# A decoder layer with hierarchical experts on one core: experts' buffers moved to multiples of 256 bytes, gathers that leave out filling rows, and LayerNorm rows kept on the chip

## The chip, the cores and the metric

The kernel runs on one core of one Trainium2 chip. The metric is the device time of one execution in microseconds (us). The kernel before took 1173.28 us as the median of 3 runs, which lay between 1173.1 and 1176.18 us. The engines are named as in the profile: PE (matrix products; PEld is its weight loading), DVE (vectors), ACT (activations), POOL, and SP, which here mostly starts transfers.

## The reference

One layer of a decoder takes one step for 512 rows of a prompt and for 32 rows of samples (8 sequences of 4): 544 rows of width 1024, all in fp32. Cut to what matters:

```
z = x @ w_in + b_in
A = mLSTM(z)          # 4 heads, chunks of 64 tokens; projection w_a
B = window attention  # 16 query heads, window 128; projection w_b
merge = (sigmoid(g_a) * A + sigmoid(g_b) * B) @ w_out
x = LN1(alpha * x + merge)
x = LN2(alpha * x + MoE(x))
x = LN3(alpha * x + sigmoid(x @ w_pg) * (p @ w_pp))

MoE(x): top-1 of 4 groups, then top-2 of the 8 experts in the group
  y += weight * ((silu(xb @ w_gate[e]) * (xb @ w_up[e])) @ w_down[e])
```

There are 32 experts. Each has a gate matrix and an up matrix of 1024 x 512 and a down matrix of 512 x 1024, 2 MB each, so 6 MB an expert. The 544 rows choose two experts each: 1088 rows pass through experts. `ln_g` and `ln_b` hold the gain and the shift of the three norms, three rows of 1024 (4 KB) each.

## The kernel before

**The stages.** The first 610 us of the span are the dense part: the projections, the two mixers and the merge. Its weights come through a ring of buffers in a pool on the right side of SBUF (`stage`), and each product runs as three products of rounded parts (L612 to L614). A planner orders this part and the tail, from a simulated time line and from hints (`tc.issue_after`). From 610 to 653 us the routing is made: scores, the chosen experts, and for every chosen row a *place*. From 653 to 1081 us the experts run, in `expert_phase`. The rest, to 1173 us, is the tail: the experts' results are gathered back, LN2, the embedding gate and LN3 follow.

**Places and items.** An expert's rows fill items of 32 places, and the last item of an expert is filled up. With these inputs there are 50 items. The routing makes `tok`, an int32 tile of 128 x 20: column g holds the token of each of the 128 places of items 4g to 4g+3. It comes out of matmuls (`At` times `Bf`, the latter holding `tokid`, the token's number), and a place that only fills an item gets the sum zero and so token 0. One gather (`gather_rows`, L228, on POOL) reads the 128 rows of four items from `x1d` in DRAM into `xg`; the first gather, L1968, stands ahead of the stage and reads by column 0 of `tok`.

**The expert stage.** Here the order on every engine is written by hand, with semaphores, in one critical section that the planner doesn't touch. There are four weight slots (`NB = 4`). Slots 0 and 1 are the tiles `w0` and `w1` on the left side of SBUF. Slot 2 is `w2a` on the left with two tiles on the right, slot 3 lies on the right and uses `r_p` for its down matrix. A slot's tile `W0` or `W1` is 12 rows of 1024 floats wide, and after the experts its rows hold other things (`row(W1, i)`).

- SP loads for each expert the gate and up matrices in halves and the down matrix in halves (L127, L133), as the slots come free.
- POOL gathers four items' rows, and stores the results of each item into `ybuf` in DRAM (L234).
- PE transposes the four items' rows (L263) into `psX`; for each item it makes gate and up products (L270), transposes h (L275), and makes the down product (L284).
- ACT applies LN1's gain and shift to the transposed rows (L370, from `gcol`), and Silu (L383). DVE copies the item's columns to `xT` (L413), multiplies h, copies hT (L418) and the result `ysb` (L425).

**Behind the last expert.** SP ends its list with the loads in `late`, one list per slot, each behind the slot's last down product (L202): half of the gate weights `w_pg` into slot 0 (2 MB, semaphore `al`), the rows of `ln_g` and `ln_b` into row 4 of slot 1 (`gb_rows`, six partitions of 4 KB, semaphore `gr`), and the four tiles of the norm's input back into `r_p` (4 x 512 KB, semaphore `rb`). PE then spreads four of these six rows over 128 partitions, each in two halves of 512 columns: a matmul with a column of the identity broadcast over 128 columns as weights (L360). It waits for `gr` first, and from the third half on for ACT's copy out of the bank two halves before (L398). DVE applies gain and shift to the first two tiles of `r_p` (L476), after the `sc` counts of their copies. The stage ends when PE, ACT, DVE and POOL have each counted up `fin`, and the loads of `al` and the stores have landed.

**The tail.** POOL gathers the results of tile 0 and tile 1 (`gather`, L1993), and SP loads the second half of `w_pg` behind the first of these. DVE splits `w_pg` into two parts (`split_from`, L2147). `affine` multiplies a tile by LN1's gain and adds its shift (L2021, L2022); `moe_norm(t)` adds the two experts' results to tile t (`both_rows`, L2026 and L2027) and normalises; `turn(t)` transposes; `embed_norm(t)` makes the gate product and LN3. The spreads of LN3's gain and shift run there too (L2008), from the same six rows.

Of the kernel before, what the change touches and what calls it, by code (L numbers as in the profile page):

```python
# [9 lines left out]
F32 = mybir.dt.float32  # L10
# [3 lines left out]
I32 = mybir.dt.int32  # L14
# [5 lines left out]
P = 128  # L20
# [31 lines left out]
def _layout(parts):  # L52
    off, o = {}, 0
    for name, n in parts:
        off[name] = (o, o + n)
        o += n
    return off, o
# [3 lines left out]
UP32, UP128 = 1.5 * 2.0 ** 28, 1.5 * 2.0 ** 30  # L61


KEEP, KEEP_N = _layout([
    ("ident", 128), ("delta", 32), ("tri", 128), ("iota", 128), ("valid", 5), ("tokid", 5), ("pcol", 1),
    ("turns", 16),
# [17 lines left out]
def _constants():  # L84
    keep = np.zeros((P, KEEP_N), np.float32)
    mix = np.zeros((P, MIX_N), np.float32)
    rel = np.zeros((NB_REL, REL_N), np.float32)

    def put(a, off, name, v):
        lo, hi = off[name]  # L90
        v = np.asarray(v, np.float32)
        a[: v.shape[0], lo:hi] = v

    p, f = np.arange(P)[:, None], np.arange(P)[None, :]
    put(keep, KEEP, "ident", p == f)
    put(keep, KEEP, "delta", (p % NS) == np.arange(NS)[None])
    put(keep, KEEP, "tri", p < f)
    put(keep, KEEP, "iota", np.broadcast_to(f, (P, P)))
    t5 = np.arange(5)[None, :]
    ok = (t5 < 4) | (p < NS)  # L100
    put(keep, KEEP, "valid", ok)
    put(keep, KEEP, "tokid", np.where(ok, t5 * P + p, 0))
    put(keep, KEEP, "pcol", p)
    put(keep, KEEP, "turns", np.broadcast_to(NB * np.arange(16)[None], (P, 16)))
    put(mix, MIX, "cmask", np.where(p <= f, 0.0, BIG))
    s, l = p % NS, np.arange(NS)[None]
    put(mix, MIX, "cmasks", np.where((s // ST == l // ST) & (s <= l), 0.0, BIG))
    put(mix, MIX, "bmk", s // ST == np.arange(SB)[None])
    put(mix, MIX, "qmask", np.broadcast_to(
        (np.arange(SB)[:, None] == np.arange(NS)[None] // ST).reshape(1, -1), (P, SB * NS)))  # L110
    h4 = np.arange(MH)[:, None]
    put(mix, MIX, "e4", h4 == np.arange(P)[None] // NS)
    put(mix, MIX, "i4", h4 == np.arange(MH)[None])
    dist = 255 - np.arange(384)
    inside = (dist >= 0) & (dist <= WIN)
    bucket = _rel_bucket(dist)
    put(rel, REL, "onehot", (np.arange(NB_REL)[:, None] == bucket[None]) & inside[None])
    put(rel, REL, "maskrow", np.broadcast_to(np.where(inside, 0.0, -BIG)[None], (NB_REL, 384)))
    return keep, mix, rel
# [13 lines left out]
    return eng.dma_start(out=W[s][2][:, ks], in_=w[2][bass.ds(e, 1)].rearrange("a (k p) d -> p (a k) d", p=P)[:, ks])  # L133


def expert_phase(tc, pool, psum, ident, meta, tok, x1, W, w, ybuf, spare, gcol, late, rows, spreads, xs, any_):

# [19 lines left out]
    psH = psum.tile([P, P], F32, name="psH")  # L159
    psY = psum.tile([P, 256], F32, name="psY")  # L160
    names = [f"{n}{i}" for n in ("gu", "gv", "wd", "we") for i in range(NB)]
    names += "gh gi gx tx c4 cx gu xa gr rb se sc ra sl hh th ch dn cy y0 y1 y2 y3 al fin gz".split()
    with tc.tile_critical(no_gpsimd_drain=True):
        S = {n: nc.alloc_semaphore("x_" + n) for n in names}

# [57 lines left out]
        def gather_rows(g):  # L223
            gp.wait_ge(S["tx"], g)
            gp.tensor_copy(out=idx, in_=tok[:, g:g + 1] if isinstance(g, int) else tok[:, bass.ds(g, 1)]).then_inc(S["gi"], 1)
            gp.wait_ge(S["gi"], g)
            gp.sem_inc(S["gz"], 1)
            gp.indirect_dma_start(out=xg, out_offset=None, in_=x1,  # L228
                                  in_offset=bass.IndirectOffsetOnAxis(ap=idx[:, 0:1], axis=0)).then_inc(S["gx"], 16)

        def store(i1, r):
            gp.wait_ge(S["cy"], gp.snap(i1 + 1))
# [115 lines left out]
        for s in range(NB):  # L348
            with pe.If((last - s) * (last - s) < 1):
                weights_in(pe.snap(nop - 1), s, "wd", 16)  # L350
                down(s, it, nop)

        halves = [(n, out[:, 512 * i:512 * (i + 1)], which, slice(512 * i, 512 * (i + 1))) for n, (out, which) in enumerate(spreads)
                  for i in range(2)]
        banks = [psX[:, 4 * i:4 * i + 4].rearrange("p k t -> p (k t)") for i in range(2)]
        pe.wait_ge(S["gr"], 32)
        for n, (_, _, which, cs) in enumerate(halves):
            if n > 1:
                pe.wait_ge(S["sc"], n - 1)
            pe.matmul(banks[n % 2], ident[0:6, which:which + 1].to_broadcast([6, P]), rows[:, cs], start=True, stop=True).then_inc(S["se"], 1)  # L360
        pe.sem_inc(S["fin"], 1)


# [29 lines left out]
                        item()  # L393

        act.activation(out=tiny, in_=gcol[:, 0, 0:1], func=AF.Sigmoid)
        for n, (_, out, _, _) in enumerate(halves):
            act.wait_ge(S["se"], n + 1)
            act.copy(out=out, in_=banks[n % 2]).then_inc(S["sc"], 1)  # L398
        act.wait_ge(S["sc"], len(halves))
# [83 lines left out]
def tile_decoder_step(ctx: ExitStack, tc: tile.TileContext, *aps):  # L483
# [4 lines left out]
    def pool(name, bufs=1, side="left", space=None, stack=ctx):  # L488
        if space is None:
            return stack.enter_context(tc.tile_pool(name=name, bufs=bufs, side=side, reuse_waits="tile"))  # L490
        return stack.enter_context(tc.tile_pool(name=name, bufs=bufs, space=space))
# [21 lines left out]
    E = pool("early", stack=early)  # L513

    right = ctx.enter_context(ExitStack())
    stg = pool("stage", bufs=2, side="right", stack=right)
    spart = stg.tile([P, 256], F32, name="spart", bufs=1)
    dense_ps = ctx.enter_context(ExitStack())
# [1041 lines left out]
    wleft = ctx.enter_context(ExitStack())  # L1560
    wright = ctx.enter_context(ExitStack())
    gcol8 = const.tile([P, 2, KD], F32, name="gcol8")
    WA = pool("wexp", stack=wleft)

    def halves_of(t):
# [49 lines left out]

    gp.dma_start(out=gcol8[:, 0], in_=A["ln_g"][0, 0].rearrange("(p k) -> p k", k=KD))
    gp.dma_start(out=gcol8[:, 1], in_=A["ln_b"][0, 0].rearrange("(p k) -> p k", k=KD))

    iota = K["iota"]
    minus, up128, firsts, ties = (RC.tile([P, n], F32, name=name)  # L1620
# [101 lines left out]
    yidx = const.tile([P, 2, NT5], I32, name="yidx")  # L1722
    smp4 = const.tile([NS, 4], F32, name="smp4")
    meta = const.tile([1, P], I32, name="meta")
    tok = const.tile([P, 20], I32, name="tok")

    wsum = const.tile([P, NT5], F32, name="wsum")
    yidxq = const.tile([P, 2], I32, name="yidxq")
# [8 lines left out]
    with ExitStack() as scope:  # L1737
# [164 lines left out]
        for i in range(2 * NT5):  # L1902
            with tc.issue_after(behind_pm.ins):
                product = pe.matmul(pt, At[:, i], Bf[:, i], start=i == 0, stop=i == 2 * NT5 - 1)
        tokens = dve.tensor_copy(out=tok, in_=pt)
        for n in (1, 2):
            product = embed(n, product)
        with tc.issue_after(behind.ins):
# [38 lines left out]
    gain1, shift1, gain2, shift2 = (row(W1, i) for i in range(4))  # L1947
    gain3, shift3 = row(W1, 11), row(w2a, 2)

    gb_rows = row(W1, 4)[0:6]  # L1950

    gbq = [row(W1, 4)[:, 0:512], row(W1, 4)[:, 512:], row(w2a, 3)[:, 0:512]]
    gbq = [t.rearrange("p (j d) -> p j d", j=2) for t in gbq]
    yall = [row(W1, i) for i in range(5, 11)] + [row(w2a, i) for i in range(2)]
# [1 line left out]
    r_back = lambda t: (r_p[:, t], x1d[t * P:(t + 1) * P])  # L1956
    late = [
        [(*pg_half(0), "al")],
        [(gb_rows[3 * j:3 * j + 3], A[n][0], "gr") for j, n in enumerate(("ln_g", "ln_b"))],
        [],  # L1960
        [(*r_back(t), "rb") for t in range(NT)],
    ]
    spreads = [(gain1, 0), (shift1, 3), (gain2, 1), (shift2, 4)]
    with ExitStack() as scope:

        SP_ = pool("spare", stack=scope)
        spare = SP_.tile([P, D], F32, name="xg"), SP_.tile([P, 2, KD, P], F32, name="xg4")
        gp.indirect_dma_start(out=spare[0], out_offset=None, in_=x1d[:], in_offset=bass.IndirectOffsetOnAxis(ap=tok[:, 0:1], axis=0))  # L1968
        expert_phase(tc, pool("xwork", side="right", stack=scope), pool("expp", space=PSUM, stack=scope), ident, meta, tok,
                     x1d[:], w_tiles, w_e, ybuf[:], spare, gcol8, late, gb_rows, spreads, x1s[:2],  # L1970
                     keep[:, 0:256])


# [29 lines left out]
    def spread(out, i):  # L2003

        for half in range(2):
            cs = slice(512 * half, 512 * (half + 1))
            po = ps2.tile([P, 512], F32, name="po")
            m = pe.matmul(po, ident[0:6, i:i + 1].to_broadcast([6, P]), gb_rows[:, cs], start=True, stop=True)  # L2008
            act.copy(out=out[:, cs], in_=po)
        return m  # L2010

# [113 lines left out]
    for k in range(KD):  # L2125
        cast = split_from(pg(k, 0, 0, 512), pg(k, 1, 0, 512), pg_in[0][:, k])
    with tc.issue_after(busy.ins), tc.issue_after(cast.ins):
        third = affine(x1s[2], gain1, shift1)
        spread(gain3, 2)
        busy = spread(shift3, 5)  # L2130
    keep_busy(8, busy)
    with tc.issue_after(dma.ins):
        for j, m in enumerate((A["ln_g"], A["ln_b"])):
            for i in range(3):
                sy.dma_start(out=gbq[i][:, j], in_=m[0, i].partition_broadcast(NS).rearrange("t (q d) -> q t d", q=4))
    with tc.issue_after(third.ins):
        behind, applied = moe_norm(0)
    with tc.issue_after(behind.ins):
        gather(2)
# [8 lines left out]
    for t in range(1, NT + 2):  # L2148
        if t <= NT:
            if t == 1:  # L2150
                for i in range(2):
                    gp.indirect_dma_start(out=yq[:, i], out_offset=None, in_=ybuf[:].rearrange("r (q d) -> (r q) d", q=4),
                                          in_offset=bass.IndirectOffsetOnAxis(ap=yidxq[:, i:i + 1], axis=0))
            if t < NT:
                with tc.issue_after(applied.ins if t > 1 else lows.ins):
                    if t == NT - 1:
                        affine(x1s[t], gain1, shift1)
                    behind, applied = moe_norm(t)
            if t == NT - 2:
                with tc.issue_after(applied.ins):  # L2160
                    moe_norm_q()
            if t == NT:
                embed_norm_q()
        if t > 1:
            embed_norm(t - 2)
        if t < NT:
            turn(t)
# [33 lines left out]
```

## Time and profile before

| | |
|---|---|
| median of 3 runs | 1173.28 us (1173.1 to 1176.18) |
| the profiled execution | 1174.74 us, its span 1173.1 us |
| mean granted clock of PE | 0.964 |
| busy over the span | PE 1051.4 us (90%), PEld 816.5 (70%), DVE 493.3 (42%), ACT 326.6 (28%), POOL 229.1 (20%) |
| moved by DMA | 277.05 MB, mean 236 GB/s |
| dense part, 0 to 610 us | PE busy 598.65 us, 139 GB/s |
| routing, 610 to 653 us | PE busy 40.73 us, 354 GB/s |
| experts, 653 to 1081 us | PE busy 340.70 us, 387 GB/s |
| tail, 1081 to 1173 us | DVE busy 76.92 us, PE 71.36 us, 122 GB/s |

The span is the time from the first to the last instruction of the profiled execution; the execution's own time has a little more around it. The page cuts the span into 40 slices of 29.3 us and gives for each the busy share of an engine in tenths (9 is 90% or more), the clock that PE was granted, the share of the 16 DMA engines and the GB/s moved. A row of the time line reads: start, length, engine, line, operation, out<-in, count, and in brackets the idle time before it and what ended it.

### The profile page before, as it was taken

How to read it: one execution, taken by the hardware profiler on the slowest of the kernel's cores; microseconds unless marked ns; L12 is line 12 of the kernel's file. 1: busy time of each engine (PE TensorE's matmuls, PEld its weight loads, DVE VectorE, ACT ScalarE, POOL GpSimd, SP SyncE). 2: the span in 40 equal slices, each digit the busy share in tenths (PEclk: the TensorE clock that was granted, in tenths of full speed). 3: DMA queues.
4: the chain of work that ended last, by engine and by line, in shares of the span. 5: the costliest groups of instructions: out<-in, count | busy, mean ns of one | idle time of the engine just before them, and what ended most of it. 6: DMA issues, size and time to landing. Idle time of an engine off the chain costs nothing.

```text
span 1173.1 us, 26748 instructions
## 1 busy us (share of the span) xinstructions
PE 1051.4 (90%) x10299; PEld 816.5 (70%) x10300; DVE 493.3 (42%) x1246; ACT 326.6 (28%) x667; POOL 229.1 (20%) x325
## 2 busy tenths in 40 slices
PE   7999999999999999999999877658999697976796
PEld 6988999999877779889988444324555354533574
DVE  3645543455555545555666311111111111112987
ACT  4411223232545645332213111011112011122310
POOL 4000001301445643014201111001112011100301
PEclk9999999999999999999999999889999899996998
DMA  8542533235114435563598899999999999993802
GB/s 247 141 137 62 159 118 94 78 93 170 55 54 145 131 103 174 144 170 92 197 408 341 300 410 413 415 412 411 410 413 411 411 411 412 412 409 105 291 8 77
DMA packets 112996, 277.05 MB, mean 236 GB/s; under 512 B 15265, under 2 KB 71687, under 8 KB 99069
## 3 DMA queue, kind: packets, MB, share of 16 engines
q1 hardware_dynamic: 92236, 238.10, 55.0%
q0 software_dynamic: 15280, 33.59, 8.2%
q10 hardware_dynamic: 5408, 4.38, 1.3%
q8 instruction: 48, 0.79, 0.3%
q14 instruction: 24, 0.19, 0.0%
HBM read 248.43 MB, written 29.57 MB: 237 GB/s over the span
## 4 chain that ended last, share of the span: by engine, by line
PE 64%; DMA 16%; SPq 12%; DVE 5%; issue 2%; ACT 0%; POOL 0%; DVEq 0%; ACTq 0%; POOLq 0%
PE pj L612 13%; PE pj L614 12%; PE pj L613 12%; SPq L127 8%; DMA w2b<-in_w_eu_dram 6%; PE psG L270 6%; DMA gu3b<-in_w_eu_dram 4%; SPq L133 3%; PE psY L284 3%; PE tp L1221 2%; PE sp L1267 1%; PE nm L1255 1%; PE psX L360 1%; DMA raw<-in_w_a_dram 1%; PE sp L672 1%
## 5 line engine op out<-in xcount | busy, mean ns | idle before, releaser
L612 PE MATMUL pj<-xH,wH 128*128 128x256 f32 (+1 forms) x672 | 198.3, 295 | 0.0
L614 PE MATMUL pj<-xH,wL 128*128 128x256 f32 (+1 forms) x672 | 197.3, 294 | 0.0
L613 PE MATMUL pj<-xL,wH 128*128 128x256 f32 (+1 forms) x672 | 196.3, 292 | 0.0
L525 ACT CAST wH<-raw 128x1024 fp32r<-128x1024 f32 x76 | 79.6, 1049 | 236.1 <-PE pj L613 151.2
L612 PEld LDWEIGHTS pj<-xH,wH 128*128 128x128 f32 x672 | 126.7, 189 | 6.3 <-issue 4.9
L614 PEld LDWEIGHTS pj<-xH,wL 128*128 128x128 f32 x672 | 126.4, 188 | 4.7 <-issue 4.3
L613 PEld LDWEIGHTS pj<-xL,wH 128*128 128x128 f32 x672 | 126.7, 189 | 2.7 <-issue 2.2
L526 DVE TENSOR_TENSOR wL<-raw,wH 128x1024 fp32r<-128x1024 f32 x76 | 94.9, 1250 | 73.0 <-ACT wH L525 72.8
L270 PE MATMUL psG<-w,xT 128*32 128x256 f32 x1216 | 74.8, 387 | 22.6 <-issue 11.7
L383 ACT ACTIVATE sg<-psG 128x128 f32<-128x128 f32 x50 | 13.9, 278 | 281.3 <-PE psG L270 281.3
L418 DVE COPY hT<-psH 128x128 f32<-128x128 f32 x50 | 14.6, 292 | 170.9 <-PE psH L275 170.9
L270 PEld LDWEIGHTS psG<-w,xT 128*32 128x32 f32 x1216 | 39.2, 111 | 50.0 <-issue 29.5
L234 POOL DMA_DIRECT2D ybuf<-ysb x50 | 35.1, 704 | 153.8 <-DVE ysb L425 149.8
L1243 POOL TENSOR_SCALAR lg<-lg,sm 128x256 f32<-128x256 f32 (+1 forms) x64 | 56.5, 897 | 28.3 <-DVE sm L1240 17.2
L413 DVE COPY xT<-xg 128x256 f32 (+1 forms) x50 | 14.7, 295 | 109.7 <-PE psG L270 109.4
L270 PE MATMUL psG<-gu3a,xT 128*32 128x256 f32 x544 | 35.9, 407 | 20.9 <-DMA gu3a<-in_w_eu_dram 14.9
L370 ACT ACTIVATE xg<-psX,gcol 128x128 f32 (+1 forms) x100 | 36.4, 468 | 45.0 <-PE psX L263 45.0
L612 PE MATMUL pj<-wH,xH 128*128 128x256 f32 x160 | 47.2, 295 | 0.0
L270 PE MATMUL psG<-w2a,xT 128*32 128x256 f32 x448 | 31.7, 431 | 17.0 <-DMA w2a<-in_w_eu_dram 11.3
L614 PE MATMUL pj<-wH,xL 128*128 128x256 f32 x160 | 45.1, 282 | 0.0
L613 PE MATMUL pj<-wL,xH 128*128 128x256 f32 x160 | 44.9, 280 | 0.0
L270 PEld LDWEIGHTS psG<-gu3a,xT 128*32 128x32 f32 x544 | 19.5, 116 | 35.3 <-issue 29.1
(589 smaller groups left out, 2257.2 us busy)
## 6 DMA issues: line engine op xcount, KB each, us to landing
w<-in_w_eg_dram SPq DMA_DIRECT2D x28, 1024.0 KB
w<-in_w_eu_dram SPq DMA_DIRECT2D x28, 1024.0 KB
w<-in_w_ed_dram SPq DMA_DIRECT2D x28, 1024.0 KB, 25.2
raw<-in_w_in_dram SPq DMA_DIRECT2D x22, 1024.0 KB
w2d<-in_w_ed_dram SPq DMA_DIRECT2D x14, 1024.0 KB, 25.7
r_p<-in_w_ed_dram SPq DMA_DIRECT2D x12, 1024.0 KB, 23.4
ybuf<-zero SPq DMA_DIRECT2D x16, 576.0 KB
w2a<-in_w_eg_dram SPq DMA_DIRECT2D x7, 1024.0 KB
```

The source lines that it names most:

```text
L127: return [eng.dma_start(out=W[s][half][:, i], in_=w[i][bass.ds(e, 1)].rearrange("a (p k) f -> (a p) k f", p=P)[:, ks]) for i in range(2)]
L133: return eng.dma_start(out=W[s][2][:, ks], in_=w[2][bass.ds(e, 1)].rearrange("a (k p) d -> p (a k) d", p=P)[:, ks])
L234: gp.dma_start(out=ybuf[bass.ds(i1 * 32, 32)].rearrange("t (c d) -> c t d", c=4), in_=ysb[:, r]).then_inc(S[f"y{r}"], 16)
L270: m = pe.matmul(psG[32 * q:32 * q + 32], xT[:, k], W[s][half][:, :, kh, P * q:P * q + P], start=k == 0, stop=k == KD - 1)
L284: m = pe.matmul(psY[32 * q:32 * q + 32], hT[:, 32 * k:32 * k + 32], W[s][2][:, k, 256 * q:256 * q + 256], start=k == 0, stop=k == 3)
L370: m = act.activation(out=out, in_=psX[:, k], func=AF.Identity, bias=gcol[:, 1, k:k + 1], scale=gcol[:, 0, k:k + 1])
L525: act.copy(out=H, in_=src)
L526: return eng.tensor_tensor(out=L, in0=src, in1=H.bitcast(F32), op=ALU.subtract)
L612: pe.matmul(out, lh(k), rh(k), start=start and i == 0, stop=False)
L613: pe.matmul(out, lh(k), rl(k), start=False, stop=False)
L614: pe.matmul(out, ll(k), rh(k), start=False, stop=stop and i == len(ks) - 1)
L1243: gp.tensor_scalar(out=lg[:, par, j, 0:nk], in0=lg[:, par, j, 0:nk], scalar1=sm[:, 2, par, j:j + 1], scalar2=None, op0=ALU.mult)
```

## The change

1. **Buffers' places in SBUF.** A tile `edge` of 224 bytes per partition at the bottom of the right side, and on the left `gb` (512 bytes), `edgel` (32 bytes) and `tok0` (32 bytes with its padding), move the four weight slots, which began 192 bytes (left) and 224 bytes (right) past a multiple of 256, to multiples of 256. What else is allocated above `edge` moves with it.
2. **Gathers.** `tokid` holds the token's number less 1000, and 1000 is added when `tok` is made from the sums. A filling place so gets 1000. The gathers of L228 get the bound 543 and skip indices beyond it (`bounds_check`, `oob_is_err=False`). The first gather goes by `tok0`, which is column 0 of `tok` with 1000 brought down to 543, so it reads all its 128 rows.
3. **LN rows.** The two loads behind slot 1's last down product and the semaphore `gr` go. Instead, POOL loads `ln_g` and `ln_b` into `gb` beside the loads of `gcol8`: 48 partitions (24 for each) of 128 floats. A spread of 512 columns (`spread_half`) is now four matmuls with 48 rows and 128 columns each, one for each 128 columns of the row, both in the stage and in the tail. PE begins them right behind the last down product.
4. **The third tile's affine step** stood ahead of `moe_norm(0)`; now it stands ahead of `moe_norm(2)`, like tile 3's ahead of `moe_norm(3)`.

```diff
-    put(keep, KEEP, "tokid", np.where(ok, t5 * P + p, 0))
+    put(keep, KEEP, "tokid", np.where(ok, t5 * P + p - NONE, 0))     # NONE = 1000
...
+def spread_half(pe, ident, rows, out, first):
+    n = rows.shape[0]
+    for k in range(4):
+        m = pe.matmul(out[:, P * k:P * (k + 1)], ident[0:n, first + k:first + k + 1].to_broadcast([n, P]), rows[:], start=True, stop=True)
+    return m
...
             gp.indirect_dma_start(out=xg, out_offset=None, in_=x1,
-                                  in_offset=bass.IndirectOffsetOnAxis(ap=idx[:, 0:1], axis=0)).then_inc(S["gx"], 16)
+                                  in_offset=bass.IndirectOffsetOnAxis(ap=idx[:, 0:1], axis=0),
+                                  bounds_check=SEQ + NS - 1, oob_is_err=False).then_inc(S["gx"], 16)
...
-        pe.wait_ge(S["gr"], 32)
-        for n, (_, _, which, cs) in enumerate(halves):
+        for n, (_, which) in enumerate(halves):
             if n > 1:
                 pe.wait_ge(S["sc"], n - 1)
-            pe.matmul(banks[n % 2], ident[0:6, which:which + 1].to_broadcast([6, P]), rows[:, cs], start=True, stop=True).then_inc(S["se"], 1)
+            spread_half(pe, ident, rows, banks[n % 2], which).then_inc(S["se"], 1)
...
+    pool("edge", side="right").tile([P, 56], F32, name="edge")
     stg = pool("stage", bufs=2, side="right", stack=right)
...
     gcol8 = const.tile([P, 2, KD], F32, name="gcol8")
+    gb = const.tile([6 * KD, P], F32, name="gb")
+    const.tile([P, 8], F32, name="edgel")
...
+    for j, n in enumerate(("ln_g", "ln_b")):
+        gp.dma_start(out=gb[24 * j:24 * j + 24], in_=A[n][0].rearrange("i (k d) -> (i k) d", k=KD))
...
-    tok = const.tile([P, 20], I32, name="tok")
+    tok, tok0 = const.tile([P, 20], I32, name="tok"), const.tile([P, 1], I32, name="tok0")
...
-        tokens = dve.tensor_copy(out=tok, in_=pt)
+        dve.tensor_scalar(out=tok0, in0=pt[:, 0:1], scalar1=float(NONE), scalar2=SEQ + NS - 1.0, op0=ALU.add, op1=ALU.min)
+        tokens = dve.tensor_scalar(out=tok, in0=pt, scalar1=float(NONE), scalar2=None, op0=ALU.add)
...
     late = [
         [(*pg_half(0), "al")],
-        [(gb_rows[3 * j:3 * j + 3], A[n][0], "gr") for j, n in enumerate(("ln_g", "ln_b"))],
+        [],
         [],
         [(*r_back(t), "rb") for t in range(NT)],
     ]
-    spreads = [(gain1, 0), (shift1, 3), (gain2, 1), (shift2, 4)]
+    spreads = [(gain1, 0), (shift1, 24), (gain2, 8), (shift2, 32)]
...
-        gp.indirect_dma_start(out=spare[0], ..., in_offset=bass.IndirectOffsetOnAxis(ap=tok[:, 0:1], axis=0))
+        gp.indirect_dma_start(out=spare[0], ..., in_offset=bass.IndirectOffsetOnAxis(ap=tok0[:, 0:1], axis=0))
...
-            m = pe.matmul(po, ident[0:6, i:i + 1].to_broadcast([6, P]), gb_rows[:, cs], start=True, stop=True)
+            m = spread_half(pe, ident, gb, po, i + 4 * half)
...
-        third = affine(x1s[2], gain1, shift1)
-        spread(gain3, 2)
-        busy = spread(shift3, 5)
+        spread(gain3, 16)
+        busy = spread(shift3, 40)
     keep_busy(8, busy)
...
-    with tc.issue_after(third.ins):
+    with tc.issue_after(cast.ins):
         behind, applied = moe_norm(0)
...
-                    if t == NT - 1:
+                    if t > 1:
                         affine(x1s[t], gain1, shift1)
                     behind, applied = moe_norm(t)
```

More of the change, by code (lines that the diff above doesn't have):

```diff
@@ L61 @@
 UP32, UP128 = 1.5 * 2.0 ** 28, 1.5 * 2.0 ** 30
+NONE = 1000
 KEEP, KEEP_N = _layout([
@@ L161, in expert_phase @@
     names = [f"{n}{i}" for n in ("gu", "gv", "wd", "we") for i in range(NB)]
-    names += "gh gi gx tx c4 cx gu xa gr rb se sc ra sl hh th ch dn cy y0 y1 y2 y3 al fin gz".split()
+    names += "gh gi gx tx c4 cx gu xa rb se sc ra sl hh th ch dn cy y0 y1 y2 y3 al fin gz".split()
     with tc.tile_critical(no_gpsimd_drain=True):
@@ L351, in expert_phase @@
                 down(s, it, nop)
-        halves = [(n, out[:, 512 * i:512 * (i + 1)], which, slice(512 * i, 512 * (i + 1))) for n, (out, which) in enumerate(spreads)
-                  for i in range(2)]
+        halves = [(out[:, 512 * i:512 * (i + 1)], which + 4 * i) for out, which in spreads for i in range(2)]
         banks = [psX[:, 4 * i:4 * i + 4].rearrange("p k t -> p (k t)") for i in range(2)]
-        pe.wait_ge(S["gr"], 32)
-        for n, (_, _, which, cs) in enumerate(halves):
+        for n, (_, which) in enumerate(halves):
             if n > 1:
                 pe.wait_ge(S["sc"], n - 1)
-            pe.matmul(banks[n % 2], ident[0:6, which:which + 1].to_broadcast([6, P]), rows[:, cs], start=True, stop=True).then_inc(S["se"], 1)
+            spread_half(pe, ident, rows, banks[n % 2], which).then_inc(S["se"], 1)
         pe.sem_inc(S["fin"], 1)
@@ L395, in expert_phase @@
         act.activation(out=tiny, in_=gcol[:, 0, 0:1], func=AF.Sigmoid)
-        for n, (_, out, _, _) in enumerate(halves):
+        for n, (out, _) in enumerate(halves):
             act.wait_ge(S["se"], n + 1)
@@ L1948, in tile_decoder_step @@
     gain3, shift3 = row(W1, 11), row(w2a, 2)
-    gb_rows = row(W1, 4)[0:6]
     gbq = [row(W1, 4)[:, 0:512], row(W1, 4)[:, 512:], row(w2a, 3)[:, 0:512]]
@@ L1967, in tile_decoder_step @@
         spare = SP_.tile([P, D], F32, name="xg"), SP_.tile([P, 2, KD, P], F32, name="xg4")
-        gp.indirect_dma_start(out=spare[0], out_offset=None, in_=x1d[:], in_offset=bass.IndirectOffsetOnAxis(ap=tok[:, 0:1], axis=0))
+        gp.indirect_dma_start(out=spare[0], out_offset=None, in_=x1d[:], in_offset=bass.IndirectOffsetOnAxis(ap=tok0[:, 0:1], axis=0))
         expert_phase(tc, pool("xwork", side="right", stack=scope), pool("expp", space=PSUM, stack=scope), ident, meta, tok,
-                     x1d[:], w_tiles, w_e, ybuf[:], spare, gcol8, late, gb_rows, spreads, x1s[:2],
+                     x1d[:], w_tiles, w_e, ybuf[:], spare, gcol8, late, gb, spreads, x1s[:2],
                      keep[:, 0:256])
```

## The prediction

> **What bounds the kernel now.** I read the page's slices first, then a table of stretches, then the chain of waits, then the timeline where the chain breaks.
>
> ```profile
> span 1173.1 us, 26748 instructions
> PEclk9999999999999999999999999889999899996998
> DMA  8542533235114435563598899999999999993802
> GB/s 247 141 137 62 159 118 94 78 93 170 55 54 145 131 103 174 144 170 92 197 408 341 300 410 413 415 412 411 410 413 411 411 411 412 412 409 105 291 8 77
> ```
>
> A slice is 29.3 us. Slices 24 to 36 show DMA at 9 and GB/s near 411: the expert stage moves weights without a gap. In slice 37 the rate falls to 105, and the DMA engines rest while the program is not yet done. The table of stretches puts numbers to both (columns: stretch, its us, busy us of each engine, granted clock, DMA share, GB/s).
>
> ```profile
> 690.00:1060.00 370.00, 296.91 (x4671) 166.00 (x4660) 57.22 (x189) 63.45 (x154) 47.80 (x71) 0.95 1.02 411
> 685.00:690.00 5.00, 3.98 (x60) 2.43 (x56) 0.91 (x3) 1.63 (x5) 0.62 (x2) 1.00 1.02 424
> 895.00:900.00 5.00, 4.70 (x85) 2.76 (x88) 1.21 (x4) 0.28 (x1) 0.00 (x0) 1.00 1.01 394
> 1060.00:1070.00 10.00, 3.65 (x5) 1.54 (x6) 0.00 (x0) 0.59 (x1) 0.00 (x1) 0.58 0.35 127
> 1070.00:1080.00 10.00, 10.00 (x13) 3.44 (x11) 4.72 (x4) 3.52 (x6) 0.00 (x0) 0.50 0.00 0
> ```
>
> From 690 to 1060 the DMA engines are full (1.02) and PE is busy 297 of 370 us: bytes set this stage. From 1070 to 1080 DMA moves nothing, PE is busy throughout, and its clock stands at 0.50. The chain of waits and the timeline of that place:
>
> ```profile
> 1026.05 24.07 DMA w2b<-in_w_eu_dram
> ...
> 1055.61 10.69 DMA w<-in_ln_b_dram
> 1066.35 14.03 PE psX L360 x16
> 1080.40 0.59 ACT w L398
> ...
> 1083.75 5.36 DMA w<-ybuf,yidx
> 1089.17 10.68 DMA w<-in_w_pg_dram
> ```
>
> ```profile
> 1056.15 1.93 PE L284 MATMUL psY<-w2d,hT 128*32 128x256 f32 x32 [1.01 <-DVE hT L418]
> 1059.32 0.69 POOL L234 DMA_DIRECT2D ybuf<-ysb  x1 [3.54 <-DVE ysb L425]
> 1066.35 14.01 PE L360 MATMUL psX<-w,keep 6*128 6x512 f32 x16 [8.26 <-DMA w<-in_ln_b_dram]
> 1070.85 2.36 DVE L476 TENSOR_TENSOR r_p<-r_p,w 128x1024 f32<-128x1024 f32 x2 [12.28 <-ACT w L398]
> 1081.73 5.58 PE L2017 MATMUL pp<-keep 128*128 128x256 f32 x16 [1.37 <-SPq L163]
> ```
>
> The last down product ends at 1056.15 + 1.93 = 1058.1. PE then waits 8.26 us for six rows of 4 KB that were queued last, behind 4 MB of other loads, and spreads them in 14.0 us at half clock: 8 halves of 1.75 us. The stage ends with the last ACT copy, 1080.4 + 0.6 = 1081.0.
>
> **The change, part by part.**
>
> LN rows. Two loads and SP's wait for slot 1 go; two loads of 12 KB join POOL's queue early, by the same kind as gcol's, and change no wait there: the next POOL work is for the tail of the input transposes. The spreads can begin behind the last down product, at about 1058.3. Each half becomes four matmuls of 128 columns, eight instructions. What else must end by then:
>
> ```profile
> w<-in_w_pg_dram SPq DMA_DIRECT2D x1, 2048.0 KB, 20.1
> r_p<-x1d SPq DMA_DIRECT2D x4, 512.0 KB, 19.1
> ybuf<-ysb POOLq DMA_DIRECT2D x50, 128.0 KB, 10.2
> L202 SPq DMA_DIRECT2D w<-in_w_pg_dram x1: 1339/1339/1339, 1045.8 to 1045.8; - x1
> 627.37 1.71 PE sp L1709 x16
> 1087.25 3.77 PE L2008 MATMUL po<-w,keep 6*128 6x512 f32 x8
> ```
>
> The gate weights land at 1045.8 + 20.1 = 1065.9: that is the floor. (The last y store, 1059.3 plus less than its median 10.2 in a draining queue, falls at about the same time; DVE's four passes of 1.18 us need the first and second pair of halves, and end near 1066 too.) PE's price: L1709 shows 16 instructions with 128-column weights in 1.71 us, 0.107 each, so eight are 0.86 us; L2008, the same spread with ACT's copies between two banks at full clock, took 3.77 for 4 halves, 0.94 each. I take the longer, 8 x 0.94 = 7.5. At full clock the spreads end at 1065.8, with the copy 1066.5: a gain of 14.5. At half clock throughout it is 8 x 1.75 = 14.0, end 1073, gain 8. PE comes warm out of the down products, but L360 ran 14 us without a gap and stayed at 0.50, so thin matmuls may not hold the clock; the new ones have 48 rows, not 6. If four halves are fast and four slow, the end is 1058.3 + 4 x 0.94 + 4 x 1.75 + 0.6 = 1069.7, gain 11. I take 13, between full and mixed, and keep 8 and 14.5. [...]
>
> Gathers.
>
> ```profile
> L228 POOL DMA_INDIRECT xg<-x1d,idx x12: 972/1032/1034, 664.2 to 1002.9; - x12
> L418 DVE COPY hT<-psH 128x128 f32<-128x128 f32 x50 | 14.6, 292 | 170.9 <-PE psH L275 170.9
> 880.80 1.03 POOL L228 DMA_INDIRECT xg<-x1d,idx  x1 [0.82 <-POOL idx L225]
> 906.07 0.18 POOL L225 COPY idx<-tok 128x1 int32 x1 [11.42 <-PE psX L263]
> 651.64 1.12 POOL L1761 DMA_DIRECT2D pld<-plo  x2
> 652.19 0.18 DVE L1905 CAST tok<-sp 128x20 int32<-128x20 f32 x1 [0.40 <-PE sp L1904]
> ```
>
> 50 items of 32 places hold 544 x 2 = 1088 rows. The twelve gathers of L228 fetch 12 x 128 = 1536 rows. The first four items hold few rows (experts 0 to 3 are chosen 12 times by these inputs), so 1076 of the 1536 are wanted and 460 only fill. 460 x 4 KB = 1.88 MB, at 411 GB/s 4.6 us; eleven of the twelve lie in the full stretch: 4.2 us. Bytes set the stage, so it is path. Bounds: 0, if the queue moves them all the same, and 4.6. The first gather still takes all 128 rows, through tok0: a second cast of 0.18 us (L1905), hidden, since POOL is busy with two stores until 652.8.
>
> 256-byte places. All the stage's loads now start 192 (left) or 224 bytes (right) past a multiple of 256, by the allocation; no load in the trace starts on one, so the price can only be bounded. Below, 0: an even start moves no more bytes. Above: the fastest five-us stretch gives 424 GB/s, and 370 x (1 - 411/424) = 11.3 us. I take 0, because the same uneven places gave 394 and 424 within one stage: something other than the start moves the rate there. The dense phase's loads are shifted too, but there DMA is not full (slices 1 to 19: 247 at most). [...]
>
> The tail.
>
> ```profile
> 1087.65 1.21 DVE L2021 TENSOR_TENSOR r_p<-r_p,w 128x1024 f32<-128x1024 f32 x1
> 1088.89 1.22 DVE L2022 TENSOR_TENSOR r_p<-r_p,w 128x1024 f32<-128x1024 f32 x1
> 1090.04 1.28 DVE L2026 SCALAR_TENSOR_TENSOR r_p<-w,wts,r_p 128x1024 f32<-128x1024 f32 x1
> 1100.53 4.91 DVE L2147 TENSOR_TENSOR pg<-w,pg 128x512 fp32r<-128x512 f32 x8 [1.42 <-DMA w<-in_w_pg_dram]
> 1139.43 0.27 DVE L1662 BATCH_NORM_AGGREGATE lmv<-pp 128x2 f32<-128x24 f32 x1 [3.49 <-PE pp L2086]
> ```
>
> The affine of the third tile (2.43 us) leaves the place before moe_norm(0). That norm then waits for its rows, landed at 1083.75 + 5.36 = 1089.1, and starts 0.9 earlier; but L2147 waits for the second half of the gate weights, which hang on the gather and not on DVE, so nothing is gained there (at best 0.9). The 2.43 us come back before moe_norm(2), where DVE is full from 1100 to 1136, ahead of the idle 3.49 us at 1139.43: PE's products set that stretch, so the idle takes them. Without it they cost 2.4. I take 0. The two spreads in the tail (0.94 to 0.86 per half) cost nothing.
>
> Sum: 1173.1 - 13 - 4.2 = 1155.9 of span. The profiled execution took 1174.74 us with what lies around the span, 1.46 over the median of 1173.28; so the median becomes 1173.28 - 17.2 = 1156.1.
>
> **The rivals.**
>
> 1. Even places pay. For it: the stage is full of DMA, so any rate counts whole. Against: the scatter 394 to 424 with the places fixed. Up to 11.3 off: 1145. Chance 0.22.
> 2. Filling rows cost nothing less, or PE holds half clock all through the spreads: 1156.1 + 4.2 = 1160, or + 5 = 1161; both 1165. Chance 0.12 for one or both.
> 3. The checked gathers cost POOL more. L228 waits for PE's transposes and its rows are needed at the next ones, 906.0 - 880.8 = 25 us later; landing takes 8.5 of them. From 1.03 us each the instruction may grow by some 16 us unseen. Beyond that PE waits twelve times: 12 x 1.5 us eats the 17, so from about 18.5 us a gather the kernel is slower; at 20, 1156 + 12 x 3 = 1192. [...] Against: 128 checks would have to take 135 ns each, where 128 addresses are now made in 1.03 us. Chance 0.04.
>
> **How the numbers follow.** The forecast (13 and 4.2 both come, the rest near 0) has 0.62 and lies at 1151 to 1161 by the bounds 14.5 + 4.6 + 0.9 and 11 + 4.2 - 2.4. To reach 8 in 10 the range goes down past rival 1 and up to rival 2's sum: 1144 to 1165. About 0.3% (3.5 us) is what a measurement of this kernel can tell from no change. Faster than that: forecast, 1, 2 = 0.95 with a rest for mishaps between; same 0.01; slower 0.04.
>
> **What would show it.** Right: L360's successor begins within 1 us of the last L284, with no idle put down to a load; the L1993 gather comes 12 to 15 us sooner after that L284 than the 24.3 of now; the software queue moves some 1.9 MB less; GB/s from 690 on stays at 408 to 415. Wrong: GB/s at 420 or more there (rival 1); L228 far over 1.03 us (3); the clock at 0.50 under the spreads (2). What I could not see is how the planner reorders the dense phase after the added loads: a few us there either way would spoil the sum without touching a step.

## The result, and the profile after

The changed kernel takes 1154.03 us as the median of 4 runs (1152.47 to 1157.61), the kernel before 1173.95 us as that of its 4: a ratio of 0.9832, 95% interval 0.9805 to 0.9859, or 20 us less. Five more runs on another chip gave 0.9832 again (0.9806 to 0.9858). The forecast was 1156. The profiled execution was the slowest of its four, 1157.61 us with a span of 1154.1; so parts are compared by spans, 19.0 us apart.

The page of the changed kernel, in the same order as before: span, granted clock, DMA share and rate in 40 slices (28.9 us each), packets, the software queue.

```profile
span 1154.1 us, 26903 instructions
PEclk8999999999999999999999999898999999987898
DMA  7542543234214433464398899999999999996601
GB/s 245 140 139 69 148 117 116 79 95 139 89 38 147 133 108 132 171 174 109 121 415 321 325 387 418 420 419 425 420 418 420 419 423 420 419 420 218 241 0 78
DMA packets 113047, 275.17 MB, mean 238 GB/s; under 512 B 15758, under 2 KB 72204, under 8 KB 99120
q0 software_dynamic: 15344, 31.73, 7.8%
```

The plateau stands at 418 to 425 GB/s; before it stood at 409 to 415. The software queue moved 31.73 MB; before, 33.59. One stretch of the full stage in both kernels, the kernel before first (columns: stretch, its us, busy us of PE, PEld, DVE, ACT and POOL, granted clock, DMA share, GB/s):

```profile
700.00:1035.00 335.00, 273.13 (x4315) 153.11 (x4303) 52.79 (x175) 58.29 (x143) 42.27 (x63) 0.95 1.02 412
```

```profile
700.00:1035.00 335.00, 279.58 (x4398) 156.73 (x4389) 53.54 (x177) 58.18 (x143) 44.29 (x65) 0.96 1.02 421
1046.00:1049.50 3.50, 3.50 (x33) 3.50 (x33) 1.28 (x2) 1.75 (x3) 0.69 (x1) 1.00 0.78 290
1049.50:1056.50 7.00, 6.95 (x33) 6.66 (x32) 3.70 (x4) 2.35 (x5) 0.00 (x0) 0.50 0.10 38
```

DMA is as full as before (1.02), at 421 GB/s. The last two rows are the spreads: full clock at first, then half, with PE busy in both. The chain of waits of the changed kernel shows what follows (start, us, what):

```profile
1013.69 22.77 DMA w2b<-in_w_eu_dram
1036.50 3.28 PE psG L283 x32
...
1043.85 1.93 PE psY L297 x32
...
1045.78 10.69 PE psX L143 x64
1056.49 0.59 ACT w L409
...
1059.87 5.29 DMA w<-ybuf,yidx
1065.22 14.34 DMA w<-in_w_pg_dram
```

The spreads (L143) follow the last down product (L297) without a gap; the 10.69 us that the chain spent on the rows of `ln_b` are gone. At the end the second half of the gate weights takes 14.34 us, where it took 10.68. DVE, which splits that half into two parts, stood idle 6.23 us ahead of it (1.42 before):

```profile
1080.24 4.91 DVE L2163 TENSOR_TENSOR pg<-w,pg 128x512 fp32r<-128x512 f32 x8 [6.23 <-ACT pg L2161]
```

The span falls into four parts. Their ends are the starts of these rows of PE and POOL, the kernel before first, and the ends of the last down products (1056.15 + 1.93 before, 1043.85 + 1.93 after):

```profile
665.99 3.66 PE L270 MATMUL psG<-w,xT 128*32 128x256 f32 x64
1082.42 1.03 POOL L1993 DMA_INDIRECT w<-ybuf,yidx  x1 [22.42 <-SPq L163]
```

```profile
663.83 3.66 PE L283 MATMUL psG<-w,xT 128*32 128x256 f32 x64
1058.54 1.03 POOL L2010 DMA_INDIRECT w<-ybuf,yidx  x1 [10.84 <-SPq L175]
```

| part of the span, us | before | after | difference |
|---|---|---|---|
| to the first gate product | 666.0 | 663.8 | -2.2 |
| first gate product to the last down product's end | 392.1 | 382.0 | -10.1 |
| from there to the first gather of the tail | 24.3 | 12.8 | -11.6 |
| from that gather to the end | 90.6 | 95.6 | +5.0 |

The forecast had 0, -4.2, -13 and 0 in this table.

### The profile page after: what moved, and what is told of

Same layout as the page of the kernel before. It is cut to its first block, busy times and chain, and to the rows that moved or that the text cites. A ratio compares the mean times of both kernels' runs of the same rounds, so it can differ in the third digit from the quotient of the medians.

```text
span 1154.1 us, 26903 instructions
## 1 busy us (share of the span) xinstructions
PE 1048.1 (91%) x10371; PEld 825.4 (72%) x10372; DVE 493.0 (43%) x1247; ACT 326.3 (28%) x667; POOL 230.9 (20%) x327
## 2 busy tenths in 40 slices
DMA packets 113047, 275.17 MB, mean 238 GB/s; under 512 B 15758, under 2 KB 72204, under 8 KB 99120
## 3 DMA queue, kind: packets, MB, share of 16 engines
q0 software_dynamic: 15344, 31.73, 7.8%
## 4 chain that ended last, share of the span: by engine, by line
PE 67%; DMA 15%; SPq 9%; DVE 6%; issue 3%; POOL 0%; ACT 0%; DVEq 0%; ACTq 0%; POOLq 0%
PE pj L625 13%; PE pj L627 13%; PE pj L626 13%; PE psG L283 8%; SPq L130 6%; DMA w2b<-in_w_eu_dram 6%; DMA gu3b<-in_w_eu_dram 4%; PE psY L297 4%; PE tp L1234 2%; SPq L136 2%; PE sp L1280 1%; PE nm L1268 1%; DMA w<-in_w_pg_dram 1%; DMA raw<-in_w_a_dram 1%; PE sp L685 1%
## 5 line engine op out<-in xcount | busy, mean ns | idle before, releaser
L283 PE MATMUL psG<-w,xT 128*32 128x256 f32 x1216 | 75.0, 388 | 21.1 <-issue 11.6
L436 DVE COPY ysb<-psY 128x256 f32<-128x256 f32 x50 | 21.2, 425 | 49.7 <-PE psY L297 49.7
```

The costliest lines, as they stand in the source:

```text
L283: m = pe.matmul(psG[32 * q:32 * q + 32], xT[:, k], W[s][half][:, :, kh, P * q:P * q + P], start=k == 0, stop=k == KD - 1)
```

## The experiments

The kernel before ran beside each group. Over the traces of all kernels the first part of the table lay anywhere between 662.5 and 670.0 us and followed none of the edits (662.5 with the places at 128, 670.0 at 224, 667.2 with only the affine step moved back). So beside each ratio stands the time from the first gate product to the end, one trace each: 507.1 us for the kernel before, 490.3 and 491.0 for the changed one.

**The standard.**

> The changed kernel again, as the standard for the kernels beside it: 1154 us, 0.983 of the kernel before. Its tail (from the stage's end to the end of the span) 97 us against 92 before, if that of the first trace was no chance; 92 if it was.

Measured: 0.9832 (0.9806 to 0.9858). The tail was 96.4 us, so the longer tail of the first trace was not chance.

**The places undone.**

```diff
-    pool("edge", side="right").tile([P, 56], F32, name="edge")
-    const.tile([P, 8], F32, name="edgel")
```

> The changed kernel with the weight slots 224 bytes past a multiple of 256 (edge and edgel taken out), all else as changed. Theory P (the even places made the stage's transfers faster): the rate between 690 and 1035 us falls from 421 back to 411 or 412 GB/s, the last down product ends 8 us later, and the time is 1162. Theory G (the rate rose because the gathers move less): the rate stays at 420 and the time is 1154, within 1.

Measured: 0.9917 (0.9885 to 0.9949); from the first gate product 499.6 us. The stretch of this kernel:

```profile
700.00:1035.00 335.00, 276.66 (x4359) 155.24 (x4356) 53.48 (x177) 58.22 (x144) 43.63 (x64) 0.94 1.02 411
```

411 GB/s, with all else as changed: theory P. First gate to last down product took 391.2 us against 382.0, where 8 us more had been expected. In the trace's packet records the 8 KB packets of this stretch took 317 ns on the mean, as in the kernel before; in the changed kernel 310. The 4 KB packets of SP's queue took 165 against 160.

**The places alone, on the kernel before.**

```diff
+    pool("edge", side="right").tile([P, 56], F32, name="edge")
...
+    const.tile([P, 16], F32, name="edgel")
```

> The kernel before with nothing but the even places (edge, and 64 bytes on the left). Theory P: 421 GB/s against 412, 8 KB packets at 310 ns, the last down product 8 us sooner, time 0.993 of the kernel before. If the places also help the dense part: another 2 to 5 us, 0.990. If they need the other parts of the change to pay: 1.000.

Measured: 0.9877 (0.9851 to 0.9903), 14 us, which is more than any of the three expectations had; from the first gate product 496.1 us. Its stretch and its chain:

```profile
700.00:1035.00 335.00, 280.56 (x4388) 156.50 (x4380) 53.53 (x178) 58.27 (x143) 43.64 (x65) 0.95 1.02 421
```

```profile
1045.02 8.63 DMA w<-in_ln_b_dram
1053.69 14.03 PE psX L360 x16
```

The rate is 421, and the last down product comes 384.2 us after the first gate product (392.1 before). PE's wait for the LN rows also shrank, by 3.5 us. Why the rows then landed closer behind the last product was not taken apart. These two make the 11 us that the trace shows from the first gate product on. Where the other 3 us of the ratio lie is not shown: the profiled execution, at 1162.47 us, lay 2.4 us above the median, and the dense part scatters by more than that. In the changed kernel the wait for the rows doesn't exist, which may be why undoing the places there costs less (10 us by the ratios) than adding them here brings; the intervals don't part the two.

**Half way.** `edge` 24 and `edgel` 40 floats wide put all slots 128 bytes past a multiple of 256.

```diff
-    pool("edge", side="right").tile([P, 56], F32, name="edge")
+    pool("edge", side="right").tile([P, 24], F32, name="edge")
...
-    const.tile([P, 8], F32, name="edgel")
+    const.tile([P, 40], F32, name="edgel")
```

> The changed kernel with all weight slots 128 bytes past a multiple of 256. If only multiples of 256 are fast: 411 GB/s between 700 and 1035 us, 8 KB packets at 317 ns, time 0.990 to 0.992, like the places at 224. If multiples of 128 (or 64) are enough: 421 GB/s, 310 ns, 0.983.

Measured: 0.9911 (0.9885 to 0.9936); from the first gate product 498.2 us.

```profile
700.00:1035.00 335.00, 276.60 (x4352) 155.18 (x4356) 52.62 (x175) 58.27 (x143) 43.71 (x64) 0.95 1.02 412
```

412 GB/s, and 316 ns for 8 KB: 128 bytes past a multiple of 256 was not enough. Beside the 310 ns on a multiple of 256, the 8 KB packets took 2.3% longer at 224 (317 ns) and 1.9% at 128; the 4 KB packets took about 3% longer at both places (165 and 164 ns against 160). Why a packet takes longer there was not shown.

**No row skipped.**

```diff
-NONE = 1000
+NONE = 0
```

> The changed kernel with NONE = 0: the bound on the gathers stays, but filling places hold token 0 again, so no row is skipped. Theory P: 460 rows or 1.88 MB come back, 4.5 us at 420 GB/s: rate 420, time 1158.5. Theory G: rate 411 and some 12 us more, 1166. If the queue moved skipped rows all the same: 1154, and the software queue's bytes as in the changed kernel.

Measured: 0.9844 (0.9819 to 0.987); from the first gate product 493.1 us, 2 to 3 more than with the skip. Its packets and queue, to be read beside those of the changed kernel:

```profile
DMA packets 113047, 277.05 MB, mean 240 GB/s; under 512 B 15298, under 2 KB 71744, under 8 KB 99120
q0 software_dynamic: 15344, 33.62, 8.3%
```

The count of packets is the same, 113047; with the skip 460 more are under 512 B and 1.88 MB fewer are moved. So a skipped row stays in the queue as a packet of a few bytes (4 B and 9 ns each, by the packet records), and the 460 rows are those counted beforehand. Of DMA time the skip saves what was forecast: SP's queue went from its 90th to its 229th MB in 355.9 us with it and 359.6 without, 3.7 less. The last down product came 2.6 to 3.1 us sooner by the traces. Two more pairs of traces differ in the gathers up to that point. With the places undone against the kernel before, the queue took 364.2 us against 367.2 and the last down product came 0.9 us sooner (391.2 against 392.1); the changed kernel against the places alone, 355.9 against 359.5 and 2.2 us. So all three pairs agree on 3 to 4 us of DMA time, and less of it, 0.9 to 3.1, reached the last down product. The medians differ by 1.7 us, and their intervals hold 0 as well as 4.2. Theory G falls: the rate is 421 here too.

```profile
700.00:1035.00 335.00, 280.73 (x4376) 156.69 (x4376) 53.48 (x177) 58.17 (x143) 44.31 (x65) 0.94 1.02 421
```

**The rows late again.** The changed kernel with `gr`, its two loads and the spreads of six rows put back (the edits of part 3 reversed).

```diff
-        [],
+        [(gb_rows[3 * j:3 * j + 3], A[n][0], "gr") for j, n in enumerate(("ln_g", "ln_b"))],
...
+        pe.wait_ge(S["gr"], 32)
```

> The changed kernel with the LN rows loaded behind slot 1's last down product again, the wait for gr and the spreads of six rows by 512 columns, in the stage and in the tail. Theory L (the wait and the slow spreads were the whole of it): from the last down product to the end of the stage 23 us against 11.3, time 1154 + 11.7 = 1165.7. Theory T (an earlier end of the stage is paid back in part by a tail 5 us longer): the tail is back at 92, and the time is 1160.7.

Measured: 0.9927 (0.9902 to 0.9953), 11.9 us over the changed kernel by the medians; from the first gate product 504.9 us. The wait and the slow spreads are back:

```profile
1047.23 10.20 DMA w<-in_ln_b_dram
1057.48 14.03 PE psX L373 x16
```

From the last down product to the first gather 24.8 us, against 12.2 to 12.8: theory L. The tail stayed long (99.0), so its length doesn't come from the stage's earlier end.

**The affine step back.**

```diff
+        third = affine(x1s[2], gain1, shift1)
         spread(gain3, 16)
...
-    with tc.issue_after(cast.ins):
+    with tc.issue_after(third.ins):
         behind, applied = moe_norm(0)
...
-                    if t > 1:
+                    if t == NT - 1:
                         affine(x1s[t], gain1, shift1)
```

> The changed kernel with the third tile's affine step back ahead of moe_norm(0). Theory A (moe_norm(0) now runs some 2 us sooner after its rows, and lets the gathers of tiles 2 and 3 go while the second gate half is still in flight; the two share the DMA engines): from issue to landing the second gate half takes 11 us against 14.3, the tail from its first gather is back at 91 against 96, and the time is 0.979 of the kernel before, 5 us under the changed kernel. Theory B (the longer tail comes from elsewhere): the tail stays at 95 to 96 and the time at 0.983.

Measured: 0.9788 (0.9763 to 0.9812), 5 us faster than the whole change; from the first gate product 485.6 us, the tail 92.4. The place to read is POOL's time line, where the gathers of tiles 2 and 3 begin, beside the chain's row for the gate half. First the changed kernel (the half was issued at 1065.22):

```profile
1069.58 1.00 POOL L2010 DMA_INDIRECT w<-ybuf,yidx  x1 [0.19 <-issue]
```

Then this one:

```profile
1073.67 1.00 POOL L2010 DMA_INDIRECT w<-ybuf,yidx  x1 [0.19 <-issue]
```

```profile
1067.37 11.39 DMA w<-in_w_pg_dram
```

The gathers start 4.4 us behind the load there and 6.3 us here, and the load takes 14.34 there and 11.39 here. While it ran in the changed kernel, the DMA engines were full (share 1.00 from 1065.2 to 1079.6 us).

**The gathers held back**, with the affine step where the change put it.

```diff
-    with tc.issue_after(behind.ins):
-        gather(2)
-        gather(3)
     high, low = turn(0)
...
             lows = dve.tensor_tensor(out=L, in0=src, in1=H.bitcast(F32), op=ALU.subtract)
+    with tc.issue_after(lows.ins):
+        gather(2)
+        gather(3)
```

> The changed kernel, the affine step where the change put it, but the gathers of tiles 2 and 3 held back until the second gate half is split. Theory A (they compete with that load): it takes 10.6 to 11.4 us from issue to landing against 14.1 to 14.3, the tail from its first gather is 91 to 92 us against 95.6 to 96.4, time 0.980. Theory O (the moved DVE work itself is what costs): the load lands sooner too, but the tail stays at 95 and the time at 0.983.

The edit did the opposite of what it was meant to: the planner put the four gathers earlier on POOL, ahead of those of the sample rows and of moe_norm(0)'s small step on POOL (L544). Measured: 0.9873 (0.9851 to 0.9894); from the first gate product 491.8 us. POOL's row of the first of the four, the chain's row of the gate half, and DVE's row behind L544:

```profile
1064.65 1.49 POOL L2010 DMA_INDIRECT w<-ybuf,yidx  x1 [0.31 <-issue]
```

```profile
1065.54 15.84 DMA w<-in_w_pg_dram
```

```profile
1073.31 1.42 DVE L1694 SCALAR_TENSOR_TENSOR r_p<-r_p,lmv,w 128x512 f32<-128x512 f32 x2 [3.37 <-POOL lmv L544]
```

The gathers began 0.9 us ahead of the load, which took 15.84 us, and moe_norm(0) waited 3.37 us for POOL. So neither expectation was put to its test, but the run gives one more point of a series. Over all traces in which this load stands behind the first gather:

| gathers of tiles 2 and 3 begin behind the load's issue, us | the load takes, us | kernels |
|---|---|---|
| -0.9 | 15.8 | the gathers that were to be held back |
| 4.4 | 13.6 to 15.1 | seven traces with the affine step moved |
| 6.3 to 6.8 | 10.5 to 11.4 | four with it in the old place (two of the changed kernel, the kernel before with and without even places) |

The sooner they begin, the later the gate half lands: theory A. That holding them back with the affine step moved would bring the whole 5 us was not shown, since no run held them back.

**128 rows in the spreads.**

```diff
-    gb = const.tile([6 * KD, P], F32, name="gb")
+    gb = const.tile([P, P], F32, name="gb")
...
+    gp.memset(gb, 0.0)
```

> The changed kernel with gb widened to 128 partitions, zeros in the 80 added ones, so that each matmul of a spread has 128 rows and no other edit. Theory C (matmuls with 48 rows don't count as work for the clock): the clock stays at 1.00 under the spreads, 64 matmuls take 7.8 us against 10.7, the stage ends 2.9 us sooner, and the time is 0.981. Theory D (the clock falls for the idle time ahead of the spreads): half clock from the fourth half on as in the changed kernel, time 0.983.

Measured: 0.9788 (0.976 to 0.9817); from the first gate product 485.9 us. The spreads' two stretches and the time line of PE:

```profile
1044.50:1048.50 4.00, 4.00 (x35) 4.00 (x36) 1.73 (x3) 1.92 (x4) 0.69 (x1) 1.00 0.89 338
1048.50:1052.60 4.10, 3.47 (x31) 3.27 (x29) 3.41 (x3) 2.77 (x5) 0.00 (x0) 1.00 0.24 92
```

```profile
1044.42 7.55 PE L143 MATMUL psX<-gb,keep 128*128 128x128 f32 x64
1053.60 0.67 PE L2035 MATMUL pp<-keep 128*128 128x256 f32 x2 [1.63 <-SPq L175]
```

The same 64 matmuls, with zeros for the added rows, and the clock stays at 1.00, as theory C had it. They take 7.55 us in all four traces with 128 rows, and 10.1 to 10.7 in the seven with 48. From the last down product to the tail's first gather 9.8 us, against 12.2 to 12.8. These 2.4 to 3.0 us are what the spreads explain; the ratio's 5 us is more than the 2.9 expected, and the rest, within its interval, is not explained. The stage's end is now set by the load of the first gate half, which the chain shows ending at 1032.44 + 20.50 = 1052.94.

```profile
1032.44 20.50 DMA w<-in_w_pg_dram
```

**Both.** The two edits together.

> The changed kernel with 128 rows in the spreads and the third affine step ahead of moe_norm(0). If the two gains add (0.9788 each against 0.9832): 0.974 to 0.975, the stage's end bound by the landing of the first gate half. If the one takes the other's place: 0.978.

Measured: 0.9776 (0.9751 to 0.98), median 1149.19 us: the fastest, though its interval doesn't part it from the two single edits, and it lies nearer to the expectation for one gain in the other's place (0.978) than to that for a sum. From the first gate product 482.3 us; with one edit each 485.6 and 485.9, with none 490.3 and 491.0. So by the traces, one for each edit, the two bring 8.0 to 8.7 us together and 4.4 to 5.4 each alone: most of both comes, which the ratios can't settle.

**The gate half sooner**, in two ways, both with 128 rows.

```diff
-        [(*pg_half(0), "al")],
+        [(*pg_half(i), "al") for i in range(2)],
...
-    for n, (out, src) in enumerate((pg_half(1), (embeds[:, 0:512], ...
+    for n, (out, src) in enumerate(((embeds[:, 0:512], ...
```

> 128 rows in the spreads, and both gate halves loaded by the list behind the last expert. The stage then ends 5 us later (2 MB at 420 GB/s; the first half's landing set its end already with 128 rows), and the tail loses the wait for the second half, at most the 6.5 us that DVE then sat idle. If the stage's end decides: 0.982; if the two cancel: 0.979; if DVE's idle time all goes: 0.977.

```diff
-            tc.add_manual_dep(dma.ins, landed.ins.name, ..., reason="behind the first rows")
```

> 128 rows in the spreads, and the second gate half started at the stage's end instead of behind the landing of tile 0's first gather. 2 MB then go beside 1 MB of gathers, 7.5 us together at 420 GB/s: the half lands some 10 us sooner than with 128 rows alone. If the gathers get their share (landing 1 or 2 us later): tail 90, time 0.975. If they stand behind the 2 MB (5 us later): 0.979 or more.

Measured: 0.9811 (0.9788 to 0.9835) and 0.9813 (0.9791 to 0.9836): neither better than 128 rows alone (0.9788), the first between two of its expectations (0.979 and 0.982); from the first gate product 485.8 and 487.9 us against 485.9. With both halves in the list the stage ended later, with its first gather 11.6 us behind the last down product instead of 9.8, and the tail took 90.0 us against 95.0. The load in the chain, which ends at 1057.34, stands ahead of that gather (1058.67):

```profile
1033.26 24.08 DMA w<-in_w_pg_dram
```

Without the dependency the gather stood beside the 2 MB and landed after 9.14 us (5.18 with 128 rows alone), as the worse of the two expectations had it:

```profile
1057.26 9.14 DMA w<-ybuf,yidx
```

## Why the prediction was right, and where its steps failed

The total came out within 2 us by luck: a gain of 8 us or more from the even places, taken as 0, stood against a loss of 5 us in the tail, also taken as 0, and against two gains that were taken too large. Two of the prediction's own signs of being wrong appeared: 421 GB/s in the stage, where 408 to 415 was to show it right, and the clock at 0.50 under the second half of the spreads. One bound is off in its own working: 14.5 + 4.6 + 0.9 below 1173.28 is 1153, not 1151.

- **LN rows: right in kind, 1.4 us too much.** Taken 13, measured 11.6 (24.3 to 12.8), and 11.9 by undoing it. The mixed case, with four halves at full clock and four at half, had 11 and is what the clock shows. The price at full clock, 7.5 us for all halves, was right too: with 128 rows it was 7.55. The step that failed is "the new ones have 48 rows, not 6" as a reason for more: 48 rows lost the full clock too (0.50 from 1049.5 to 1056.5 us), 128 kept it (1.00 from 1044.5 to 1052.6). The floor by the first gate half was named and became the bound only there.
- **Gathers: the DMA term right, the path term smaller.** 4.2 taken, 3.0 to 3.7 found in SP's queue, 0.9 to 3.1 at the last down product, 1.7 in the medians, whose intervals hold 0 as well as 4.2.
- **Even places: the wrong value of the bounds was taken.** The step that failed is "something other than the start moves the rate there". Stretches of five us scatter with what moves in them: from 690 us on the kernel before reached 405 GB/s on the mean where over a fifth of the bytes went by the software queue, and 419 where hardly any did. With even places they scatter no less, 393 to 436, around a higher mean. So 394 beside 424 said nothing of a cost on the mean packet (317 ns against 310 for 8 KB). The bound, 11.3, held: 8 to 9 us in the stage. The first rival's gain was real (421 GB/s against 412 with the places alone), and came together with the forecast's rather than in its place.
- **The tail: the failed step is "which hang on the gather and not on DVE, so nothing is gained there (at best 0.9)".** The start of the second gate half did hang on the gather. Its length hung on what ran beside it. moe_norm(0), freed of 2.4 us on DVE, let four gathers go 2 us sooner, into that load; it took 3.7 us longer. The price of moving the affine step, by undoing it, is 5 us; the most that had been allowed for it was 2.4, for its return ahead of moe_norm(2). Whether the part of the 5 us beyond the load's 3.7 lies there was not taken apart.
- **POOL:** L240, the checked gather, took 1.09 us on the median against 1.03, so the third rival fell.
- **The dense part:** the two added loads and the moved buffers left no mark beyond a scatter of 7.5 us between traces, which is larger than what was allowed for.

A busy PE did not by itself keep the full clock: with 48 rows it was busy 3.50 of 3.50 us at 1.00, and the next 7.00 us, busy for 6.95, show 0.50; with 128 rows it was busy 4.00 of 4.00 us and 3.47 of the next 4.10, both at 1.00. What the clock goes by was not shown beyond this.

## What to carry to other kernels

Where DMA is full through a stage (share 1.02 here), look for a small cost on every packet: 2 to 3% (317 ns against 310 for 8 KB, 165 against 160 for 4 KB) were worth 8 to 9 us here, beside 11.6 for the wait and the slow spreads at the stage's end. Look at where the buffers start, and measure it with a padding tile, before explaining a scatter. When work is moved away from ahead of a step, list the transfers that this step lets go and what they will run beside; here that cost 5 us of a step which by itself was free. An equal sum is no proof of its terms: only the stage-by-stage table showed two wrong ones.

## What the runs showed of the hardware that I had not expected

- 128 bytes past a multiple of 256 was nearly as slow as 224: 412 and 411 GB/s, against 421 on a multiple.
- A row that a gather skipped was still a packet: 460 packets of 4 B at 9 ns.
- Matmuls of 48 rows, back to back for 3.50 us, lost the full clock; the same 64 matmuls with 80 rows of zeros added kept it, 7.55 us for all spreads instead of 10.1 to 10.7.
